# Float32r projections: the two activation parts side by side under one weight load, and three value projections with 512 weight columns

## The chip, the cores and the metric

The kernel runs on one core of a Trainium2 chip. The metric is device time in microseconds (us), the median of several runs. TensorE (PE in the rows) multiplies, VectorE (DVE) and ScalarE (ACT) work on SBUF and PSUM, GpSimd (POOL) takes a few additions, and all large loads are issued from SyncE's queue (SPq).

## The reference, cut to what matters

`x` is [256 tokens, 1024 features], float32. The first block has two layers: layer 0 with a gated convolution beside a retention, layer 1 with a bidirectional state-space scan (S5) followed by a GLU, and each with an MLP of 4096 hidden features. The second block adds three attention-like branches, gates them, and ends in a SwiGLU. What the change touches is this:

```python
# layer 1 of the first block
mix = (z @ w_glu_a) * jax.nn.sigmoid(z @ w_glu_b)            # z = gelu(S5(h)), 1024 -> 1024
x = x + gate_m * mix
h = _rmsnorm(x, norm_g[layer, 1]) * (1.0 + scale_f) + shift_f
x = x + gate_f * (jnp.square(jax.nn.relu(h @ w_fc1[layer])) @ w_fc2[layer])   # 1024 -> 4096 -> 1024
...
# the second block: projections of rmsnorm(x) to gated linear attention (q, k, v, gate),
# to forgetting attention (q, k, v), to memory attention (q), and to 3 x 1024 gates;
# keys and values of a memory of 256 slots; three branch matrices 512 -> 1024, an output
# matrix 1024 -> 1024, and a SwiGLU of 2816 hidden features
```

## The kernel before, in words

Activations lie with a feature to a partition and 256 tokens along the free axis: `[128, 8, 256]` is a whole activation, block `k` of it 128 features. Each float32 matrix product is done with operands of type float32r, in three products. Weights and activations are each split into a high part (ScalarE copies it to float32r, L314) and a low part (VectorE subtracts, L315). `mm3` (L318 to L321) then issues three passes into the same PSUM bank: high weights by high activations, high weights by low activations, low weights by high activations. Each pass streams 256 columns and has its own weight load.

A weight piece is 1 MB, `[128, 8 blocks of 128 inputs, 256 outputs]`. `piece` loads it into one of four buffers (tag `w`) and splits it in four steps, four instructions on ScalarE and four on VectorE, into one of two buffers of high and of low parts (tags `hi`, `lo`). `lin` takes the input blocks `k` in the outer loop and the two output column blocks in the inner one, so a piece is 8 x 2 triples of passes and fills one PSUM bank of 512 columns (two blocks of 256 tokens). Tag `mm` has two such banks, `at` four, `fa` and `fp` one each. `lin_tok` has the roles exchanged: 128 tokens of the activations are the stationary operand and 256 weight columns stream; `tok` (L1154) calls it for value projections, two pieces for 512 columns.

After `lin`, one instruction over both column blocks usually reads the bank: a ReLU (L657) and a square in the MLP, a product with the per-token factor `rb` in the gates (L1290) and in SwiGLU (L1530), `Square` and `Copy` in `heads` (L1172, L1173), a gated product in the branches (L1497), an addition to `x` after `w_out2` (L1505).

The order on each engine is fixed when the program is built: a scheduler simulates the engines and takes what is ready by the order of the source. Some work is traced as fill between the steps of something else: the twelve gate pieces between the steps of the attentions, and the memory's projections (`memory`, L1211) at three places from the GLU on. In GLU the input blocks are taken in the order 0, 2, 4, 6, 1, 3, 5, 7 (`ks`, L1125), since the scan finishes the even ones first. High and low parts of an activation come from a pool `h` of two buffers of 8 KB a partition.

## Time and profile before

| | us |
|---|---|
| median of three runs | 1230.05 (1228.49 to 1230.53) |
| span of the profiled execution | 1227.2 |
| median less span | 2.85 |
| TensorE busy in the span | 1169.7 (95%) |
| VectorE busy | 891.7 (73%) |
| ScalarE busy | 609.7 (50%) |

The busy share of TensorE is the union of its passes with their pipeline time, so a stretch at 100% may still hold more or fewer passes. The span falls into a first half with much loading and scanning (to about 500 us), GLU (500 to 560 us), the second layer's MLP (580 to 770 us), the second block's attentions, branches and output matrix (770 to 1030 us) and SwiGLU (1030 to 1227 us).

### The profile page before, as it was taken

How to read it: one execution, taken by the hardware profiler on the slowest of the kernel's cores; microseconds unless marked ns; L12 is line 12 of the kernel's file. 1: busy time of each engine (PE TensorE's matmuls, PEld its weight loads, DVE VectorE, ACT ScalarE, POOL GpSimd, SP SyncE). 2: the span in 40 equal slices, each digit the busy share in tenths (PEclk: the TensorE clock that was granted, in tenths of full speed). 3: DMA queues.
4: the chain of work that ended last, by engine and by line, in shares of the span. 5: the costliest groups of instructions: out<-in, count | busy, mean ns of one | idle time of the engine just before them, and what ended most of it. 6: DMA issues, size and time to landing. Idle time of an engine off the chain costs nothing. (4 is left out here: it accounts for less than half of the span.)

```text
span 1227.2 us, 25417 instructions
## 1 busy us (share of the span) xinstructions
PE 1169.7 (95%) x10482; PEld 1109.3 (90%) x10482; DVE 891.7 (73%) x1821; ACT 609.7 (50%) x1202; POOL 106.1 (9%) x138
## 2 busy tenths in 40 slices
PE   6899897999999976899999999999999999999998
PEld 4698686999999964899999999999999999999998
DVE  7879888889888859767765656686667686665564
ACT  3577244655555542545544545573465545544441
POOL 0077321000000006200000000000000000000000
PEclk8899997999999977799999999999999999999999
DMA  9888886688888999554466655453443454555541
GB/s 341 340 311 327 297 294 212 238 265 282 297 287 267 300 249 309 216 172 171 169 243 212 233 174 172 164 172 104 151 159 138 172 168 148 194 179 177 194 155 60
DMA packets 69979, 267.29 MB, mean 218 GB/s; under 512 B 7380, under 2 KB 35428, under 8 KB 43240
## 3 DMA queue, kind: packets, MB, share of 16 engines
q1 hardware_dynamic: 69864, 265.68, 63.5%
q8 instruction: 82, 1.34, 0.4%
q14 instruction: 33, 0.27, 0.1%
HBM read 246.85 MB, written 18.81 MB: 216 GB/s over the span
## 5 line engine op out<-in xcount | busy, mean ns | idle before, releaser
L315 DVE TENSOR_TENSOR lo<-w,hi 128x512 fp32r<-128x512 f32 (+1 forms) x640 | 427.6, 712 | 147.7 <-ACT hi L314 147.1
L314 ACT ACTIVATE hi<-w 128x512 fp32r<-128x512 f32 (+1 forms) x640 | 358.4, 625 | 337.0 <-PE mm L320 118.8
L319 PE MATMUL mm<-h,hi 128*128 128x256 f32 x1328 | 379.7, 286 | 0.3 <-ACT h L398 0.3
L320 PE MATMUL mm<-h,hi 128*128 128x256 f32 x1328 | 377.7, 285 | 1.3 <-DVE h L399 1.1
L321 PE MATMUL mm<-h,lo 128*128 128x256 f32 x1328 | 378.6, 285 | 0.0
L319 PEld LDWEIGHTS mm<-h,hi 128*128 128x128 f32 x1328 | 254.7, 192 | 7.2 <-issue 3.4
L320 PEld LDWEIGHTS mm<-h,hi 128*128 128x128 f32 x1328 | 254.6, 192 | 2.8 <-DVE h L399 1.5
L321 PEld LDWEIGHTS mm<-h,lo 128*128 128x128 f32 x1328 | 254.5, 192 | 2.6 <-issue 1.6
L321 PE MATMUL at<-s,lo 128*128 128x256 f32 x720 | 204.4, 284 | 1.7 <-DVE lo L315 1.7
L319 PE MATMUL at<-s,hi 128*128 128x256 f32 x720 | 204.8, 284 | 0.0
L320 PE MATMUL at<-s,hi 128*128 128x256 f32 x720 | 204.1, 284 | 0.0
L321 PEld LDWEIGHTS at<-s,lo 128*128 128x128 f32 x720 | 137.9, 192 | 2.5 <-DVE lo L315 2.1
L319 PEld LDWEIGHTS at<-s,hi 128*128 128x128 f32 x720 | 138.0, 192 | 1.8 <-issue 1.4
L320 PEld LDWEIGHTS at<-s,hi 128*128 128x128 f32 x720 | 138.0, 192 | 0.6 <-issue 0.6
L439 PE MATMUL fa<-wa,crep 128*32 128x256 f32 x704 | 56.4, 428 | 7.0 <-DMA wa<-in_ada_dram 3.8
L537 POOL TENSOR_TENSOR s<-s,cv 128x256 f32<-128x256 f32 x60 | 49.9, 866 | 38.9 <-ACT cv L536 38.7
L439 PEld LDWEIGHTS fa<-wa,crep 128*32 128x32 f32 x704 | 23.0, 120 | 27.0 <-issue 6.4
L319 PE MATMUL fp<-h,hi 128*128 128x256 f32 x144 | 41.9, 291 | 0.7 <-ACT h L314 0.7
L320 PE MATMUL fp<-h,hi 128*128 128x256 f32 x144 | 41.8, 290 | 0.0
L321 PE MATMUL fp<-h,lo 128*128 128x256 f32 x144 | 41.6, 289 | 0.0
L929 ACT COPY Wt<-fp 128x512 f32<-128x512 f32 x32 | 18.6, 581 | 43.3 <-PE fp L928 39.9
L536 ACT ACTIVATE cv<-ap,s 128x256 f32<-128x256 f32 x60 | 29.5, 506 | 17.2 <-POOL s L537 16.4
(438 smaller groups left out, 1829.6 us busy)
## 6 DMA issues: line engine op xcount, KB each, us to landing
w<-in_fc_dram SPq DMA_DIRECT2D x64, 1024.0 KB, 5.1
wa<-in_ada_dram SPq DMA_DIRECT2D x44, 1024.0 KB, 6.5
w<-in_w_in_dram SPq DMA_DIRECT2D x38, 1024.0 KB, 4.9
w<-in_w_gate_dram SPq DMA_DIRECT2D x11, 1024.0 KB, 5.0
w<-in_w_up_dram SPq DMA_DIRECT2D x11, 1024.0 KB, 4.9
Vd<-V SPq DMA_DIRECT2D x16, 512.0 KB, 6.6
w<-in_w_out_dram SPq DMA_DIRECT2D x8, 1024.0 KB, 6.2
Wd<-Wt SPq DMA_DIRECT2D x16, 512.0 KB, 5.2
```

The source lines that it names most:

```text
L314: self.nc.scalar.activation(hi, h, AF.Copy)
L315: self.nc.vector.tensor_tensor(lo, h, hi.bitcast(F32), op=ALU.subtract)
L319: mm(ps, sh, mh, start=start, stop=False, skip_group_check=True)
L320: mm(ps, sh, ml, start=False, stop=False, skip_group_check=True)
L321: mm(ps, sl, mh, start=False, stop=stop, skip_group_check=True)
L439: nc.tensor.matmul(ps[32 * q:32 * q + 32], self.crep[:, 2 * k + k2], w[:, n:n + 256], start=k == 0 and k2 == 0, stop=k == 3 and k2 == 1, t ...
L536: nc.scalar.mul(t, src, w)
L537: nc.gpsimd.tensor_tensor(acc[:, ch], acc[:, ch], t, op=ALU.add)
L929: nc.scalar.copy(W[:, :, k], pt.rearrange("p (e x) -> p e x", e=4))
```

## The change

High and low parts of an activation now lie in one buffer, `[128, 2, 8, 256]`, so that one pass can stream both, 512 columns, under one load of the high weights. The low weights still meet the high part alone, 256 columns, and add to the first half of the bank. A bank then holds one column block in two halves, and their sum is formed on eviction: ScalarE copies the second half to SBUF and VectorE adds it to the first. `lin2` has the column block outside and the input blocks inside. It replaces `lin` in GLU, in the second layer's first MLP matrix, in the memory's keys and in all of the second block and SwiGLU but the last matrix. The first layer, both second MLP matrices, `w_down` and the small projection keep `lin` or `mm3`.

The values of the two attentions and of the memory come from weights laid out with 512 columns (`w_v`, 4 input blocks to a piece): 128 tokens are stationary, 512 weight columns stream, the two token halves in the two `mm` banks at once. In `memory` both value pieces are now one step of the fill. In `ffn` of layer 1 the ReLU is folded into VectorE's square. After `w_out2`, VectorE adds the two halves to `x` one after the other. The pool `h` has one buffer of 16 KB instead of two of 8 KB. Comments and docstrings are gone from the source; the scan's tables share the new `h` buffer.

```diff
+    w2m = np.concatenate([w2[:, :1536], w2[:, 1552:3088], w2[:, 3092:]], 1)
+    d["w_v"] = con(np.concatenate([dense(a, 512) for a in (w2m[:, 512:1024], w2m[:, 2560:3072], f(v["w_mem_kv_2"])[0][:, 512:])]))
...
-        self.vplace = ("h", "w", "hi", "hi", "lo", "h", "lo", "w")
+        self.vplace = ("h2", "w", "hi", "hi", "lo", "h", "lo", "w")
...
+    def lin2(self, W, act, kn=8, cols=(0, 1), tags=("mm", "mm")):
+        for n, c in enumerate(cols):
+            ps = self.pair(tags[n])
+            s = slice(c * 128, c * 128 + 128)
+            for k in range(kn):
+                self.nc.tensor.matmul(ps, W[0][:, k, s], act[2][:, :, k], start=k == 0, stop=False, skip_group_check=True)
+                self.nc.tensor.matmul(ps[:, 0], W[1][:, k, s], act[0][:, k], start=False, stop=k == kn - 1, skip_group_check=True)
+            yield n, ps
+
+    def summed(self, dst, W, act, tags=("mm", "mm")):
+        for c, ps in self.lin2(W, act, tags=tags):
+            self.merge(dst[:, c], ps)
+
+    def merge(self, out, ps):
+        e = self.sb([128, T])
+        self.nc.scalar.copy(e, ps[:, 1])
+        self.nc.vector.tensor_tensor(out, ps[:, 0], e, op=ALU.add)
...
+    def both(self, n=8, tag="h"):
+        a = self.sb([128, 2, n, T], F32R, tag)
+        return a[:, 0], a[:, 1], a
...
     def ffn(self, x, h, l, fill, need, each):
...
-                ps = self.pair()
-                self.lin(ps, self.piece(f"fc1_{l}", 2 * q + j), h, K8)
                 r = self.sb([128, 2, T])
-                nc.scalar.activation(r, ps, AF.Relu)
+                if l:
+                    self.summed(r, self.piece(f"fc1_{l}", 2 * q + j), h)
+                    nc.vector.scalar_tensor_tensor(r, r, 0.0, r, op0=ALU.max, op1=ALU.mult)
...
-        ks = [(k, k) for k in (0, 2, 4, 6, 1, 3, 5, 7)]
...
-            self.lin(pa, Wa, z, ks)
-            self.lin(pb, Wb, z, ks)
-            t = self.sb([128, 2, T])
-            nc.scalar.activation(t, pb, AF.Tanh, scale=0.5)
-            v.scalar_tensor_tensor(t, t, 1.0, pa, op0=ALU.add, op1=ALU.mult)
+            t, a = self.sb([128, 2, T]), self.sb([128, 2, T])
+            self.summed(a, Wa, z)
+            self.summed(t, Wb, z, ("fp", "at"))
+            nc.scalar.activation(t, t, AF.Tanh, scale=0.5)
+            v.scalar_tensor_tensor(t, t, 1.0, a, op0=ALU.add, op1=ALU.mult)
...
-    def tok(self, dst, name, js, h, rc):
-        for n, j in enumerate(js):
-            ps = self.pair()
-            self.lin_tok(ps, self.piece(name, j), h)
-            for b in range(2):
-                self.nc.scalar.activation(dst[:, b, 256 * n:256 * n + 256], ps[:, b], AF.Copy, scale=rc[:, b:b + 1])
+    def tok(self, dst, i, h, rc):
+        ps = [self.ps("mm") for _ in range(2)]
+        for k0 in (0, 4):
+            W = self.piece("w_v", i, k0, 4, 512)
+            for k in range(4):
+                for b in range(2):
+                    s = slice(128 * b, 128 * b + 128)
+                    self.mm3(ps[b], h[0][:, k0 + k, s], h[1][:, k0 + k, s], W[0][:, k], W[1][:, k], k0 + k == 0, k0 + k == 7)
+        for b in range(2):
+            self.nc.scalar.activation(dst[:, b], ps[b], AF.Copy, scale=rc[:, b:b + 1])
...
     def heads(self, dst, name, js, h, g, rc, out=None):
-            ps = self.pair()
-            self.lin(ps, self.piece(name, j), h, [(k, k) for k in range(8)])
+            self.summed(d, self.piece(name, j), h)
             sq = self.sb([128, 2, T], tag="q2")
-            nc.scalar.activation(sq, ps, AF.Square)
-            nc.scalar.activation(d, ps, AF.Copy, scale=g)
+            nc.scalar.activation(sq, d, AF.Square)
+            nc.scalar.activation(d, d, AF.Copy, scale=g)
...
     def memory(self):
-        for n in range(2):
-            self.tok(self.mv[:, :, 256 * n:256 * n + 256], "w_mkv", (2 + n,), (hh, hl), rc)
-            yield
+        self.tok(self.mv, 2, (hh, hl), rc)
+        yield
...
         def gate(i, j):
-            ps = self.pair()
-            self.lin(ps, self.piece("w_in2", 14 + 4 * i + j), h, K8)
             g = gates[i][:, 2 * j:2 * j + 2]
-            tt(g, ps, rb2, op=ALU.mult)
+            self.summed(g, self.piece("w_in2", 14 + 4 * i + j), h)
+            tt(g, g, rb2, op=ALU.mult)
...
                 for c2 in range(2):
-                    ps = self.pair()
-                    self.lin(ps, W, ys[i], [(k, k) for k in range(4)], cols=(2 * c2, 2 * c2 + 1))
+                    z = self.sb([128, 2, T])
+                    for c, ps in self.lin2(W, ys[i], 4, (2 * c2, 2 * c2 + 1)):
+                        self.merge(z[:, c], ps)
-                    v.scalar_tensor_tensor(gates[i][:, s], gates[i][:, s], 1.0, ps, op0=ALU.add, op1=ALU.mult)
+                    v.scalar_tensor_tensor(gates[i][:, s], gates[i][:, s], 1.0, z, op0=ALU.add, op1=ALU.mult)
...
-            self.lin(ps, self.piece("w_out2", j), (mh, ml), K8)
-            v.scalar_tensor_tensor(x[:, 2 * j:2 * j + 2], ps, 0.5, x[:, 2 * j:2 * j + 2], op0=ALU.mult, op1=ALU.add)
+            for c, ps in self.lin2(self.piece("w_out2", j), mx):
+                xc = x[:, 2 * j + c]
+                for a in range(2):
+                    v.scalar_tensor_tensor(xc, ps[:, a], 0.5, xc, op0=ALU.mult, op1=ALU.add)
...
     def swiglu(self, x, h, rb):
-                self.lin(pg, self.piece("w_gate", j0 + j), h, K8)
-                self.lin(pu, self.piece("w_up", j0 + j), h, K8)
+                t, u, w = (self.sb([128, 2, T]) for _ in range(3))
+                self.summed(u, self.piece("w_gate", j0 + j), h)
+                tt(u, u, bc, op=ALU.mult)
                 nc.scalar.activation(t, u, AF.Tanh, scale=0.5)
+                self.summed(w, self.piece("w_up", j0 + j), h, ("fa", "fp"))
                 v.scalar_tensor_tensor(t, t, 1.0, u, op0=ALU.add, op1=ALU.mult)
-                tt(t, t, pu, op=ALU.mult)
+                tt(t, t, w, op=ALU.mult)
...
-            self.pools = {t: pool(t, b) for t, b in (("h", 2), ("s2", self.n2), ("q2", self.nq), ("s1", self.n1), ("s0", 12))}
+            self.pools = {t: pool(t, b) for t, b in (("h", 1), ("s2", self.n2), ("q2", self.nq), ("s1", self.n1), ("s0", 12))}
```

## Rows read from the trace of the kernel before

**Rows 1.** The page: TensorE's granted clock in 40 slices, tenths.

```profile
PEclk8899997999999977799999999999999999999999
```

**Rows 2.** Windows: us, busy us (instructions) of each engine, clock, DMA, GB/s.

```profile
1100.00:1200.00 100.00, 100.00 (x836) 100.00 (x835) 55.64 (x90) 43.75 (x80) 0.00 (x0) 1.00 0.53 178
```

**Rows 3.** Timeline of TensorE in GLU: start us, duration us, instruction; 11 passes apart.

```profile
548.38 0.28 PE L319 MATMUL mm<-h,hi 128*128 128x256 f32 x1
...
549.70 0.28 PE L321 MATMUL mm<-h,lo 128*128 128x256 f32 x1
```

**Rows 4.** Groups by line and shape, TensorE from 500 us on.

```profile
L319 PE MATMUL mm<-h,hi 128*128 128x256 f32 x912 | 259.4, 285 | 0.0
...
L319 PE MATMUL fp<-h,hi 128*128 128x256 f32 x144 | 41.9, 291 | 0.7 <-ACT h L314 0.7
...
L319 PE MATMUL fa<-h,hi 128*128 128x256 f32 x96 | 27.2, 283 | 0.0
L319 PE MATMUL mm<-ys,hi 128*128 128x256 f32 x96 | 27.2, 283 | 0.0
```

**Rows 5.** Timeline of TensorE in cross attention: float32 passes (L1463), then float32r.

```profile
933.57 0.59 PE L1463 MATMUL at<-mk,s 128*128 128x256 f32 x2
934.00 0.38 PE L1438 MATMUL at<-ident,s 128*128 128x128 f32 x2
934.22 0.60 PE L1463 MATMUL at<-mk,s 128*128 128x256 f32 x2
...
934.77 0.28 PE L319 MATMUL mm<-h,hi 128*128 128x256 f32 x1
```

**Rows 6.** Timeline of TensorE in the memory's keys, ten passes apart.

```profile
571.44 0.28 PE L321 MATMUL mm<-hi,mhl 128*128 128x256 f32 x1
...
572.57 0.28 PE L319 MATMUL mm<-hi,mhh 128*128 128x256 f32 x1
```

**Rows 7.** Timeline of TensorE at GLU's start, five passes apart, and the window there.

```profile
505.22 0.41 PE L321 MATMUL fp<-h,lo 128*128 128x256 f32 x1
...
506.29 0.41 PE L320 MATMUL fp<-h,hi 128*128 128x256 f32 x1
...
504.00:509.00 5.00, 5.00 (x25) 5.00 (x24) 3.43 (x13) 2.16 (x5) 0.00 (x0) 0.50 1.01 426
```

**Rows 8.** Groups by line and shape, ScalarE and VectorE from 480 us on.

```profile
L314 ACT ACTIVATE hi<-w 128x512 fp32r<-128x512 f32 x440 | 244.3, 621 | 271.1 <-PE mm L320 101.9 <-issue 84.8 <-PE at L320 57.2
...
L1254 ACT COPY rb<-fp 128x256 f32<-128x256 f32 x1 | 0.4, 372 | 2.3 <-PE fp L369 2.3
...
L315 DVE TENSOR_TENSOR lo<-w,hi 128x512 fp32r<-128x512 f32 x440 | 280.6, 687 | 116.3 <-ACT hi L314 115.9
...
L315 DVE TENSOR_TENSOR lo<-w,hi 128x256 fp32r<-128x256 f32 x4 | 1.4, 418 | 0.0
```

**Rows 9.** Windows: the branches, and the decays with linear attention's projections.

```profile
968.00:1004.40 36.40, 36.40 (x300) 36.22 (x299) 28.56 (x49) 16.17 (x33) 0.00 (x0) 1.00 0.45 153
...
800.00:820.00 20.00, 20.00 (x166) 19.72 (x165) 17.75 (x32) 15.74 (x26) 0.00 (x0) 1.00 0.55 191
```

**Rows 10.** Timeline of VectorE at the end of the scan.

```profile
503.29 1.42 DVE L315 TENSOR_TENSOR h<-s,h 128x256 fp32r<-128x256 f32 x4
...
508.35 1.43 DVE L315 TENSOR_TENSOR h<-s,h 128x256 fp32r<-128x256 f32 x4 [1.57 <-ACT h L314]
```

**Rows 11.** Timeline of VectorE at SwiGLU's start.

```profile
1029.94 2.46 DVE L384 SCALAR_TENSOR_TENSOR h<-x,vec,h 128x256 fp32r<-128x256 f32 x6
1032.31 2.49 DVE L315 TENSOR_TENSOR lo<-w,hi 128x512 fp32r<-128x512 f32 x4
1034.72 0.88 DVE L384 SCALAR_TENSOR_TENSOR h<-x,vec,h 128x256 fp32r<-128x256 f32 x2
```

**Rows 12.** Timeline of ScalarE at the start of block two.

```profile
787.84 0.84 ACT L1161 ACTIVATE s<-mm,rc 128x256 f32<-128x256 f32 x2 [0.61 <-DVE rc L1252]
```

More of the change, by code (lines that the diff above doesn't have):

```diff
@@ L375, in rms @@
         return self.spread(self.rsqrt_eps(ms[:, :, 0]))
+    def both(self, n=8, tag="h"):
+        a = self.sb([128, 2, n, T], F32R, tag)
+        return a[:, 0], a[:, 1], a
     def gained(self, x, g):
-        hh, hl = self.sb([128, 8, T], F32R, "h"), self.sb([128, 8, T], F32R, "h")
+        act = self.both()
+        hh, hl = act[0:2]
         def make(j):
@@ L384, in make @@
                 self.nc.vector.scalar_tensor_tensor(hl[:, c], x[:, c], g[:, c:c + 1], hh[:, c].bitcast(F32), op0=ALU.mult, op1=ALU.subtract)
-        return (hh, hl), make
+        return act, make
     def col(self, name, i=0, n=1):
@@ L393, in normed @@
         nc = self.nc
-        hh, hl = self.sb([128, 8, T], F32R, "h"), self.sb([128, 8, T], F32R, "h")
+        act = self.both()
+        hh, hl = act[0:2]
         for c in range(8):
@@ L1084, in finish @@
             if ih == 0:
-                z.extend(self.sb([128, 8, T], F32R, "h") for _ in range(2))
-            zh, zl = z
+                z.extend(self.both())
+            zh, zl = z[0:2]
             for t2 in range(2):
@@ L1124, in s5 @@
         v.tensor_scalar_mul(hg, self.modv(l, 2), 0.5)
-        ks = [(k, k) for k in (0, 2, 4, 6, 1, 3, 5, 7)]
         for j in range(4):
-            pa, pb = self.pair(), self.pair("fp")
             if j == 0:
@@ L1219, in memory @@
         g = self.col("g_mem", 0, 8)
-        hh, hl = (self.memh.tile([128, 8, T], F32R, name=n) for n in ("mhh", "mhl"))
+        hx = self.memh.tile([128, 2, 8, T], F32R, name="mh")
+        hh, hl = hx[:, 0], hx[:, 1]
         for c in range(8):
@@ L1337, in block2 @@
         gv = self.sb([128, 2, 512])
-        self.tok(gv, "w_in2", (2, 3), h, rc)
+        self.tok(gv, 0, h, rc)
         gs = self.sb([128, 4, T])
         for c in range(2):
-            pg = self.pair()
-            self.lin(pg, self.piece("w_in2", 4 + c), h, K8)
             t, u = self.sb([128, 2, T]), gs[:, 2 * c:2 * c + 2]
-            tt(u, pg, rb2, op=ALU.mult)
+            self.summed(u, self.piece("w_in2", 4 + c), h)
+            tt(u, u, rb2, op=ALU.mult)
             nc.scalar.activation(t, u, AF.Tanh, scale=0.5)
@@ L1347, in block2 @@
         ki, ko = en, eo
-        ps = self.pair()
-        self.lin(ps, self.piece("w_in2", 0), h, K8)
-        v.scalar_tensor_tensor(qi, ps, 0.125, er, op0=ALU.mult, op1=ALU.mult)
-        ps = self.pair()
-        self.lin(ps, self.piece("w_in2", 1), h, K8)
-        tt(ki, ps, en, op=ALU.mult)
-        tt(ko, ps, eo, op=ALU.mult)
+        self.summed(qi, self.piece("w_in2", 0), h)
+        v.scalar_tensor_tensor(qi, qi, 0.125, er, op0=ALU.mult, op1=ALU.mult)
+        kz = self.sb([128, 2, T])
+        self.summed(kz, self.piece("w_in2", 1), h)
+        tt(ki, kz, en, op=ALU.mult)
+        tt(ko, kz, eo, op=ALU.mult)
         P = self.sb([128, 2, 2, 2, 128])
@@ L1386, in block2 @@
         fill.step(self.grate[0])
-        ys = [[self.sb([128, 4, T], F32R, "ys") for _ in range(2)] for _ in range(3)]
+        ys = [self.both(4, "ys") for _ in range(3)]
         for c in range(2):
@@ L1488, in block2 @@
         self.mark("b2.branch")
-        mh, ml = self.sb([128, 8, T], F32R, "h"), self.sb([128, 8, T], F32R, "h")
+        mx = self.both()
+        mh, ml = mx[0:2]
         for n, i in enumerate((0, 1, 2)):
@@ L1668, in build @@
             memh_pool.__exit__(None, None, None)
-            with self.phase(s8=3, s4=self.s4, l2=6, ys=6):
+            with self.phase(s8=3, s4=self.s4, l2=6, ys=3):
                 self.mark("norm2")
```

31 lines of the change are left out of this document (16 added, 15 removed).

## Prediction

> **What bounds the kernel now.** I read the stages before the totals. The page's clock row [rows 1] shows where TensorE ran at half its granted clock: near the start, around 200 us and from about 440 to 520 us, the state-space scan. The change starts after that. From 600 us on TensorE is busy all the time at full clock with 836 passes in 100 us, while VectorE is busy 56 us of it, ScalarE 44, the DMA engines 0.53 [rows 2]. Waits there don't set the end; the number of passes and what each takes do. One pass of 256 columns starts 0.120 us after the one before (11 in 1.32 us [rows 3]); its shown duration of 0.28 us overlaps its neighbours and is no price.
>
> **What is converted.** By the code a piece of 256 output columns is 8 feature blocks by 2 column blocks, 16 triples of three passes. GLU has 8 such pieces, the second layer's fc1 16, the memory's keys 2, the gates 12, linear attention's gate, q and k 4, the heads' projections 6, w_out2 4, gate and up 22; with the 6 branch pieces, also 16 triples each, that is 80 pieces, 1280 triples. The trace's groups agree: 912 + 144 + 96 + 96 and the 32 of the keys [rows 4]. A triple of 256 + 256 + 256 becomes 512 + 256: the same columns, one weight load and one pass fewer.
>
> **Price of a pass of 512.** No row has one of this type. The nearest is the float32 pass of cross attention, which streams for as long at the same clock: two take 0.43 us, and two followed by one float32r pass of 256 take 0.55 [rows 5]. So a long pass is 0.215 with its successor's weight load hidden, the short one 0.12: 0.335 for the pair against 0.360. From below, nothing beats the long row. From above: if a pass is paid by the column at the fastest rate that 256 columns show, 0.113 (ten in 1.13 us [rows 6]), 512 cost 0.226; at the usual rate, 0.240. I take 0.215, because at half clock the period is 0.214 for 256 columns [rows 7], 1.2 columns per ns, exactly the 1.2 GHz level with nothing added, while at 2.4 GHz 256 columns should need half of that, 0.107, and take 0.120. What the extra 0.013 is does not stretch with the array's clock; a weight load that isn't quite hidden behind 256 columns fits, and behind 512 it would be hidden.
>
> The Trainium skill speaks against this: "TensorE: Matmul & The Clock Gate", section "Back-to-back issue gap", gives N / 2.4 + 2.5 ns, so 109 for 256 and 216 for 512 columns; by it a triple falls only from 328 to 325 ns, and 1280 of them give 3 us. The trace agrees for the long pass (0.215) and not for the short (0.120).
>
> **Gains.** 1280 x 0.025 = 32.0 us. The three value projections go from 96 passes of 256 columns (two pieces) to 48 of 512 each: 48 x (0.240 - 0.215) x 3 = 3.6. Together 35.6 us, all in stretches at full clock but for some 5 us of GLU.
>
> **What evictions add.** Each column block now ends in a ScalarE copy out of PSUM (0.37 us) and a VectorE addition (0.42 [rows 8]), where one instruction over two blocks read PSUM before. A block is 8 pairs, 2.68 us. The chain from its last pass is 0.28 + 0.37 + 0.42 and hand-overs, near 1.2 us; its bank is wanted again one block later, 2.68 us on. So 1.5 us remain for what stands ahead in the two queues, mainly pieces of the weight split (0.62 on ScalarE, 0.69 on VectorE, four to a weight piece [rows 8]). That cover is enough where the queues have room; gate/up and GLU alternate over more banks and have more. Seven places have less:
>
> - Branches: 4 feature blocks, so a bank comes back after 1.34 us, close to the 1.2. VectorE is busy 28.6 of 36.4 us there [rows 9]; 24 more additions, 0.40 apart as short ones run in a row [rows 11], make 38, against TensorE's 96 x 0.335 plus some 2 us of attention, 34. I charge 5 us.
> - Decays and linear attention's projections: VectorE 17.75 of 20 us [rows 9]; three to four pieces bring 8 x 0.4 - with 18.6 us to do it in, 2 us over.
> - GLU's start. Before, k runs through the even blocks first, since these come from the scan early; some 24 passes ran on them at half clock [rows 7] while the odd blocks were made (low parts of the two sets from 503.3 and from 508.35 us [rows 10]). lin2 takes k in natural order, so the second pair needs an odd block: TensorE idles to about 508.4 and starts cold (0.214 a pass) what it had begun. 24 warm passes are 2.9 us: 3.
> - SwiGLU's start. lin2 runs all eight k for the first column block at 0.335 each; before, a k lasted 0.72. The normed blocks come at 0.40, the last two at 1034.7 to 1035.6, behind a weight split [rows 11]. 2 us.
> - Value projections hold both "mm" banks from start to end, then both are evicted. The three must wait for the preceding block's additions and, behind them, for a copy of 512 elements (two of 256 take 0.84 [rows 12]): 1 us each, 3.
> - The memory's values are now one step of the fill, so the second piece (its 1 MB load on SP's queue, eight split instructions, its passes) moves from 769 us, where it covered the start of block two, to about 580. There it only shifts work. At 769 TensorE runs into the last normed blocks (0.7 us), and the linear attention's values fill both banks before the per-token factor, that the eviction waits for [rows 12], is ready. 2 us.
> - Elsewhere (heads: square and scale now read the merged tile, one hop later; w_out2: two VectorE reads of each bank): 2 us.
>
> Sum 19 us. The one 16 KB buffer for high and low parts replaces two of 8 KB; both were written and freed together, so I cost it at nothing: the work that hides it is the pass that still reads the old contents, before as after. Loads keep their size; SP's queue issues as many, and 0.53 of the DMA engines leaves room. The ReLU moves from ScalarE to VectorE's squaring (same instruction count there).
>
> 35.6 - 19 = 16.6. The profiled span is 1227.2 us; the median run, 1230.05, lies 2.85 above, which I keep: span 1210.6, time **1213.5 us**.
>
> **Rivals.**
> *All hides*: the scheduler orders the evictions so well that only GLU's start and the branches cost, 8 us: 35.6 - 8 = 27.6, about 1202; with nothing lost, 1194.5. For it: before, TensorE idled for almost nothing [rows 2]. Against: the branches' VectorE sum.
> *Slower passes*: 512 columns at 0.226 to 0.227. A pair costs 0.347, the gain is 1280 x 0.013 + 144 x 0.013 = 18.5, less 19: 1230.5, no change. For it: 0.113 is also a period that rows show [rows 6].
> *Columns are the price* (other side): each column costs 0.120 / 256 whatever the pass; the gain is 0, the list stays: 1249. For it: the rows of this type all have 256 columns, so they can't exclude it. Against: the faster period of the same columns [rows 6]. The page's formula above ends here too: 3 - 19, 1246.
> *Evictions bind* (other side): if the two queues delay a merge by more than the 1.5 us on the 88 blocks outside branches that use only the two "mm" banks, each 0.3 us more is 26 us: 1240. It decides from about 0.2 us a block on. For it: VectorE's extra 0.8 us a piece brings fc1 pieces to some 5 of 5.36 us. Against: fc2 pieces between them have no merges.
>
> **Chances.** Forecast (1205 to 1222) 0.52; all hides 0.14; slower passes 0.12; columns 0.08; evictions 0.14. A measurement of this kernel tells a difference of 0.2% or more, 2.5 us, from none. Faster: 0.52 + 0.14, a third of the slower-pass case and a quarter of the eviction case, 0.74. Same 0.05. Slower 0.21. The range 1198 to 1236 leaves out half of "all hides", the column case and the worse part of the eviction case, 0.2 together. The forecast's own range is 1205 to 1222.
>
> **What would show it.** In fc1 and gate/up stretches, 512-column passes at 0.215 after their start and pairs at 0.335 (0.347 or 0.360 would be the second and third rival). TensorE idle: a gap at 500 to 509 us, one before the first gate piece, waits on VectorE's additions in the branches and next to nothing in fc1. VectorE busy near 85% from 780 us on. If pairs take 0.335 and the time is still over 1225, the list of waits was too short; if fc1's blocks wait for banks, the eviction rival holds.

## The result, and the profile after

The changed kernel takes 1274.45 us (1270.70 to 1279.25), the kernel before on the same chip 1229.27 (1226.64 to 1230.53): ratio 1.0354, 95% interval 1.0328 to 1.0381. It is 45 us slower; the forecast was 1213.5. The profiled span went from 1227.2 to 1268.9.

Four moments divide these 41.7 us: GLU's last addition to `x`, the first and the last gated product of the branches, and the end. Views of the two lines before (L1141, L1497) and after (L1176, L1534); the two times are the first and the last start:

```profile
L1141 DVE SCALAR_TENSOR_TENSOR x<-s,hgate,x x8: 714/726/776, 525.7 to 561.9; 128x256 f32<-128x256 f32 x8
L1497 DVE SCALAR_TENSOR_TENSOR s<-s,mm x12: 679/684/689, 971.6 to 1004.8; 128x512 f32<-128x512 f32 x12
L1176 DVE SCALAR_TENSOR_TENSOR x<-s,hgate,x x8: 734/754/780, 531.4 to 567.7; 128x256 f32<-128x256 f32 x8
L1534 DVE SCALAR_TENSOR_TENSOR s<-s,s x12: 685/691/693, 1001.4 to 1047.1; 128x512 f32<-128x512 f32 x12
```

GLU ends 5.8 us later; from there to the first product it is 24.0 us more; the products take 45.7 us instead of 33.2, 12.5 more; and from the last product to the end it is 0.6 less.

The page of the changed kernel, busy time by engine and the clock row, beside [rows 1]:

```profile
PE 1173.1 (92%) x9058; PEld 1039.3 (82%) x9058; DVE 954.1 (75%) x1997; ACT 657.6 (52%) x1344; POOL 107.5 (8%) x138
...
PEclk9899997999999977997999999999999999999999
```

TensorE is as busy as before with some 1400 passes fewer, and the time is longer, so two things went wrong: the passes are not cheaper as hoped, and TensorE waits. Windows of the changed kernel: GLU's start, the keys, a stretch of fc1, the start of block two, the branches and SwiGLU (columns as in [rows 2]):

```profile
504.00:510.00 6.00, 3.16 (x34) 2.04 (x23) 5.76 (x19) 2.67 (x6) 0.00 (x0) 0.75 0.92 347
570.00:582.00 12.00, 1.43 (x6) 1.05 (x6) 10.44 (x33) 5.24 (x13) 0.00 (x0) 0.58 0.28 104
600.00:700.00 100.00, 99.92 (x672) 91.60 (x672) 68.51 (x131) 49.45 (x97) 0.00 (x0) 1.00 0.58 211
800.00:840.00 40.00, 31.52 (x157) 25.12 (x156) 31.50 (x78) 28.71 (x51) 0.00 (x0) 0.96 0.36 132
1001.40:1047.10 45.70, 38.33 (x192) 30.30 (x191) 35.68 (x67) 22.96 (x51) 0.00 (x0) 0.96 0.34 115
1100.00:1200.00 100.00, 100.00 (x630) 89.87 (x629) 71.17 (x129) 56.56 (x114) 0.00 (x0) 1.00 0.52 186
```

fc1 and SwiGLU have no holes: there the evictions are covered. All the others have: 10.6 of 12 us idle at the keys, 8.5 of 40 at block two's start, 7.4 of 45.7 in the branches, where [rows 9] had none. The branches hold 192 passes as planned.

What TensorE waited for from 500 us on (us in total, times, longest):

```profile
PE mm L341 <- DVE s L353: 10.9, 13, 3.3
PE mm L341 <- DVE mk L353: 6.9, 1, 6.9
PE fp L393 <- DVE rc L1290: 4.3, 1, 4.3
PE at L393 <- DVE s L373: 3.8, 1, 3.8
PE at L1508 <- DVE s L1504: 3.3, 1, 3.3
PE mm L341 <- DVE h L318: 3.0, 2, 1.6
```

L353 is the addition in `merge`, the second half of an eviction; L341 is the 512-column pass. So the largest waits are for a bank whose eviction isn't done. At the keys the rest of the queue shows. Timelines of ScalarE and of VectorE there: both make eight normed blocks first (L429; L428, L430), and only then evict the keys' banks, which TensorE filled long before:

```profile
575.77 3.30 ACT L429 ACTIVATE h<-s,mod 128x256 fp32r<-128x256 f32 x8 [4.45 <-DVE s L428]
578.98 0.75 ACT L352 COPY s<-mm 128x256 f32<-128x256 f32 x2
```

```profile
575.25 3.22 DVE L428 SCALAR_TENSOR_TENSOR s<-x,modg,at 128x256 f32<-128x256 f32 x8 [1.32 <-PE at L393]
578.39 3.25 DVE L430 SCALAR_TENSOR_TENSOR h<-s,mod,h 128x256 fp32r<-128x256 f32 x8
581.56 0.75 DVE L353 TENSOR_TENSOR mk<-mm,s 128x256 f32<-128x256 f32 x2
```

The eviction's own two instructions were priced right (L352 0.363, L353 0.420 us, estimated from [rows 8] as 0.37 and 0.42):

```profile
L352 ACT COPY s<-mm 128x256 f32<-128x256 f32 x134 | 48.5, 363 | 52.5 <-PE mm L342 50.4 <-issue 1.4 <-DVE s L1247 0.5
...
L353 DVE TENSOR_TENSOR s<-mm,s 128x256 f32<-128x256 f32 x128 | 53.6, 420 | 10.5 <-ACT s L352 10.0
```

And the pass. TensorE's timeline in SwiGLU, eleven pairs of 512 and 256 columns apart; it answers [rows 3]:

```profile
1119.68 0.40 PE L341 MATMUL fp<-h,hi 128*128 128x512 f32 x1
1119.92 0.28 PE L342 MATMUL fp<-h,lo 128*128 128x256 f32 x1
...
1123.57 0.40 PE L341 MATMUL mm<-h,hi 128*128 128x512 f32 x1
```

Eleven pairs take 3.89 us, 0.354 each, against 0.360 for three passes before. Over all pairs at full clock the median is 0.350: 0.235 from the long pass's start to the next, 0.117 from the short one's. The forecast had 0.215 and 0.120.

### The profile page after: what moved, and what is told of

Its sections match the earlier page's. It is cut to its first block, busy times and chain, and to the rows that moved or that the text cites. A ratio compares the mean times of both kernels' runs of the same rounds, so it can differ in the third digit from the quotient of the medians.

```text
span 1268.9 us, 22899 instructions
## 1 busy us (share of the span) xinstructions
PE 1173.1 (92%) x9058; PEld 1039.3 (82%) x9058; DVE 954.1 (75%) x1997; ACT 657.6 (52%) x1344; POOL 107.5 (8%) x138
## 4 chain that ended last, share of the span: by engine, by line
PE 77%; DVE 13%; DMA 3%; ACT 3%; POOL 2%; issue 1%; SPq 0%; ACTq 0%; DVEq 0%; POOLq 0%
PE mm L341 18%; PE mm L342 9%; PE at L322 7%; PE at L323 7%; PE at L324 7%; DVE lo L318 5%; PE mm L322 4%; PE mm L323 4%; PE mm L324 4%; PE fp L341 2%; PE fa L470 2%; PE fa L341 2%; DVE fp L564 1%; PE at L170 1%; POOL s L568 1%
## 5 line engine op out<-in xcount | busy, mean ns | idle before, releaser
L318 DVE TENSOR_TENSOR lo<-w,hi 128x512 fp32r<-128x512 f32 (+1 forms) x640 | 436.6, 717 | 173.2 <-ACT hi L317 172.5
L317 ACT ACTIVATE hi<-w 128x512 fp32r<-128x512 f32 (+1 forms) x640 | 363.6, 626 | 272.2 <-PE mm L341 91.8
L341 PE MATMUL mm<-h,hi 128*128 128x512 f32 x912 | 331.4, 405 | 10.3 <-DVE s L353 4.1
L341 PEld LDWEIGHTS mm<-h,hi 128*128 128x128 f32 x912 | 173.1, 190 | 53.6 <-DVE s L353 6.2
L322 PE MATMUL mm<-h,hi 128*128 128x256 f32 x416 | 120.9, 291 | 0.3 <-ACT h L429 0.3
L323 PE MATMUL mm<-h,hi 128*128 128x256 f32 x416 | 119.6, 288 | 1.1 <-DVE h L430 1.1
L322 PEld LDWEIGHTS mm<-h,hi 128*128 128x128 f32 x416 | 80.7, 194 | 6.7 <-issue 3.1
L323 PEld LDWEIGHTS mm<-h,hi 128*128 128x128 f32 x416 | 80.7, 194 | 2.0 <-DVE h L430 1.5
L352 ACT COPY s<-mm 128x256 f32<-128x256 f32 x134 | 48.5, 363 | 52.5 <-PE mm L342 50.4
L353 DVE TENSOR_TENSOR s<-mm,s 128x256 f32<-128x256 f32 x128 | 53.6, 420 | 10.5 <-ACT s L352 10.0
```

What stands on the lines that cost most here:

```text
L317: self.nc.scalar.activation(hi, h, AF.Copy)
L318: self.nc.vector.tensor_tensor(lo, h, hi.bitcast(F32), op=ALU.subtract)
L322: mm(ps, sh, mh, start=start, stop=False, skip_group_check=True)
L323: mm(ps, sh, ml, start=False, stop=False, skip_group_check=True)
L341: self.nc.tensor.matmul(ps, W[0][:, k, s], act[2][:, :, k], start=k == 0, stop=False, skip_group_check=True)
L352: self.nc.scalar.copy(e, ps[:, 1])
```

## Experiments: what a pass costs

**Long passes cut in two.** The changed kernel with each pass of 512 as two of 256 under the same weights; evictions and banks stay.

```diff
-                self.nc.tensor.matmul(ps, W[0][:, k, s], act[2][:, :, k], start=k == 0, ...)
+                for a in range(2):
+                    self.nc.tensor.matmul(ps[:, a], W[0][:, k, s], act[a][:, k], start=k == 0 and a == 0, ...)
```

> The changed kernel with one edit: the pass of 512 columns is issued as two passes of 256 with the same high weights, into the two halves of the bank. Banks, evictions and the order of work are those of the changed kernel. It prices the wide pass alone. Theory P (columns are the price: the changed kernel's pairs take 0.350 us against 0.360 for three narrow passes): at most 1280 x 0.010 = 13 us more, less where TensorE waits anyway, so 1280 to 1288. Rival (the prediction's price, 0.025 a triple, part of it lost in waits): 25 us more or over, 1300 and up.

Measured 1281.98 us, ratio 1.0399 (1.0361 to 1.0437); the span is 11.3 us above the changed kernel's, the ratio 0.0045, 5.5 us. In 100 us of SwiGLU it starts 835 passes, as many as [rows 2]:

```profile
1100.00:1200.00 100.00, 100.00 (x835) 100.00 (x834) 73.44 (x133) 58.00 (x117) 0.00 (x0) 1.00 0.53 182
```

So 1280 long passes are worth some 5 us by the ratios, give or take 6, and 11 by the spans, not 32.

**High weights only.** Left out: the product of low weights and high activations.

```diff
-                self.nc.tensor.matmul(ps[:, 0], W[1][:, k, s], act[0][:, k], start=False, stop=k == kn - 1, ...)
```

> The changed kernel with the passes of low weights left out everywhere but in the value projections, fc2, down and the stages before GLU, so it leaves out the product of low weights and high activations: only the price of a 512-column pass behind another with other weights is read from it, at 2.4 GHz, and its time is that of less work. Columns theory (about 0.115 us per 256 columns whatever stands around them): starts 0.226 to 0.236 apart, median near 0.231. Rival, that a pass of 512 costs 0.215 and the 0.020 more in the changed kernel come from the weight load of the short pass that follows it, or of the long one behind the short: starts 0.213 to 0.219 apart. TensorE then idles between blocks, and VectorE and ScalarE set the pace in the gated stretches: the time should fall less than the 1136 short passes' 133 us, by 70 to 110 us, to 1165 to 1205.

One run, 1171.7 us. Timeline of TensorE, 16 long passes with different weights one behind the other:

```profile
1110.25 3.79 PE L341 MATMUL mm<-h,hi 128*128 128x512 f32 x16
1113.87 0.39 PE L341 MATMUL fa<-h,hi 128*128 128x512 f32 x1
```

3.62 us for 16: 0.226 each; over 1049 such intervals the median is 0.227, the tenth and the ninetieth percentile 0.226 and 0.235. That refutes 0.215. It is twice the 0.113 of [rows 6] (rows of the memory's values, weights streaming past its activations, not of its keys). It can be read in another way: at half clock this run's long passes take 0.427, so 0.213 would be their columns alone at full clock, and 0.013 is over; of the 0.120 for 256 columns the same 0.013 is over beyond 0.107. Whether the extra goes by the column or by the pass, these rows don't tell. The prediction had it gone behind 512 columns, and it is not. Beside a short pass a long one takes a little more, 0.235. The time fell by 103 us, in the range given.

## Experiments: the banks

**Branches and w_out2 alternate over two pairs of banks.**

```diff
-  for c, ps in self.lin2(W, ys[i], 4, (2 * c2, 2 * c2 + 1)):
+  for c, ps in self.lin2(W, ys[i], 4, (2 * c2, 2 * c2 + 1), (("mm", "mm"), ("at", "at"))[c2]):
...
-  for c, ps in self.lin2(self.piece("w_out2", j), mx):
+  for c, ps in self.lin2(self.piece("w_out2", j), mx, tags=(("mm", "mm"), ("at", "at"))[j % 2]):
```

> The changed kernel with one edit: in the branches and the output matrix every second piece half puts its two column blocks into two banks of tag at instead of mm, so four banks take turns. Nothing else is touched. Theory A (a bank now holds one column block, so two banks let TensorE run ahead of the evictions by half as much work as before, and it stops where a weight split stands ahead of a merge): the changed kernel's branches took 45.7 us from the first to the last gated product against 33.2 before; with four banks they should take 35 to 37, and the time fall by 9 to 12 us, to about 1263. Rival B (VectorE and ScalarE simply have too much to do after the added evictions): VectorE is busy as long as before, branches stay above 42 us, time within 4 us of 1274.

1268.23 us, 1.0287 (1.0247 to 1.0328): by the ratios some 8 us less, give or take 6, between the two expectations. The changed kernel's many small waits from 1001 to 1075 us are gone:

```profile
PE mm L341 <- DVE s L353: 7.3, 11, 0.9
```

But a single wait there has grown from 1.3 to 6.0 us. Window of the branches with four banks, and that wait (from 1002 to 1070 us):

```profile
1002.50:1042.00 39.50, 33.47 (x184) 29.10 (x183) 33.82 (x66) 22.04 (x50) 0.00 (x0) 0.93 0.39 135
```

```profile
PE mm L341 <- DVE h L318: 6.0, 1, 6.0
```

VectorE is busy 33.8 of 39.5 us; it ends its work after TensorE has, and w_out2's first operand, the low part made there, comes 6.0 us late. More banks alone don't mend a stage in which VectorE is near its limit.

**Keys into other banks.**

```diff
-  self.heads(self.mk[...], "w_mkv", (n,), (hh, hl, hx), self.col("g_mem_k"), rc)
+  self.heads(self.mk[...], "w_mkv", (n,), (hh, hl, hx), self.col("g_mem_k"), rc, tags=(("at", "at"), ("fa", "fp"))[n])
```

> The changed kernel with one edit: the memory's two key pieces put their column blocks into the banks at, at and fa, fp instead of mm, mm. In the changed kernel TensorE stands idle for 11 us between 570 and 582 us, when both mm banks hold key blocks whose merges are queued behind the norm's chain. Theory A: with banks of their own both key pieces and the values run through this chain; the gap falls under 2 us, the time by 8 to 11 us, to about 1265. Rival C (the gap is due to the values' second piece being moved or to the chain itself being later): the gap stays over 6 us, time over 1270.

1270.91 us, 1.0320 (1.0285 to 1.0356): some 4 us less, which the intervals don't tell from none, where 8 to 11 were expected. The 11 us hole at 570 to 582 is gone, and another stands at 615 us, where the head norm's factors are late (TensorE's waits from 568 to 625 us):

```profile
PE at L393 <- DVE s L1219: 4.3, 1, 4.3
```

**Memory's values last,** where a part of them stood before the change.

```diff
-        self.memat = (1, 3, 0)
+        self.memat = (1, 2, 0)
```

> The changed kernel with the memory's value projection as the last thing before block two instead of in the stretch of the second norm at 570 us. Cover theory (the 4.7 us hole at 806 us, where TensorE waits for both mm banks full of linear attention's values until the per-token factor is ready, is there because nothing is left to cover the second norm's chain): the hole goes or falls under 1 us, the stretch from ffn1's end to the first gate grows by the moved work (about 11 us of passes) less 4, the ffn1 stretch shrinks by about 11; time about 4 us under the changed kernel, 1270.5, with 1268 to 1272.5. Rival, that the factor's chain starts later when the work before it is gone, since VectorE or ScalarE sets it and not TensorE: the hole stays within 1 us and the time within 1.5 us of the changed kernel's.

1276.49 us, 1.0364 (1.0339 to 1.0389): no gain, so the cover theory falls. The wait on the per-token factor `rc` goes as it said, but others of 6.5 and 3.3 us come (its waits, 780 to 840 us). It fits that the second norm's and the decays' chains on VectorE and ScalarE are long by themselves, and that covering their beginning only shows their end; no run tests this alone:

```profile
PE at L1367 <- DVE s L1364: 6.5, 1, 6.5
PE at L1347 <- ACT l L1348: 3.3, 1, 3.3
```

**The value projections alone,** on the kernel before (`tok`, the layout `w_v`, values as one step of the fill).

> The kernel before with one part of the change: the three value projections with 512 weight columns, both token halves in the two mm banks, and the memory's values as one step of the fill. lin stays everywhere else. Theory D (this part costs by itself, since both banks wait for the per-token factor at the start of block two and the cover there was moved): 4 to 8 us slower than before, 1234 to 1238, with a gap near the first eviction of linear attention's values. Rival (it gives its 1 to 4 us of shorter passes): 1226 to 1229.

1236.92 us, 1.0041 (1.0018 to 1.0063), in the range expected, with its longest hole where TensorE waits 4.3 us for `rc`. The values fill both banks before the factor that their eviction needs is ready, as the prediction said of this step, at a higher price: 5.0 us, where its terms (3 and 2, less a gain of 3.6) gave 1.4.

## Experiments: SwiGLU alone loses, and why

**SwiGLU only.** The changed kernel with every other stage's passes, evictions and projections set back.

> The changed kernel with every stage but SwiGLU's gate and up set back to three passes of 256 columns and the old evictions and value projections; the joined buffer for high and low parts stays. Price theory (a triple saves 0.010 us, 352 triples 3.5 us, four banks hide the evictions, and the start loses under 1 us): 1226 to 1230, 2 to 5 us under the kernel before, PE idle in SwiGLU under 2 us. Rival, that the joined 16 KB buffer costs by itself because the next norm's high parts wait for the last pass that reads the old ones: at or over the kernel before, with gaps at the starts of ffn1, block two and SwiGLU. Rival, that the 5.1 us that the SwiGLU stretch was shorter in the changed kernel was a late start cut off elsewhere: within 1 us of the kernel before.

1235.64 us, 1.0028 (1.0015 to 1.0040): slower, where a gain was expected, though SwiGLU itself has no holes once it runs. The rival that the joined buffer costs by itself is the one to follow: two losses stand ahead of it. One is at its start. VectorE and ScalarE, and TensorE's timeline:

```profile
1036.08 1.15 ACT L314 ACTIVATE hi<-w 128x512 fp32r<-128x512 f32 x2 [3.98 <-issue]
1037.14 2.49 ACT L410 ACTIVATE h<-x,vec 128x256 fp32r<-128x256 f32 x6
...
1037.96 2.46 DVE L411 SCALAR_TENSOR_TENSOR h<-x,vec,h 128x256 fp32r<-128x256 f32 x6
...
1038.49 0.50 PE L338 MATMUL mm<-h,hi 128*128 128x512 f32 x1 [1.59 <-DVE h L411]
...
1039.40 0.63 PE L338 MATMUL mm<-h,hi 128*128 128x512 f32 x1
...
1041.32 0.63 PE L338 MATMUL mm<-h,hi 128*128 128x512 f32 x1
```

Two weight splits go ahead of the first normed blocks on ScalarE, and VectorE starts its blocks at 1037.96 behind the same two; in [rows 11] the blocks come first. The hole is small, but behind it three pairs take 1.92 us, 0.64 each, instead of 1.05: TensorE stands at its 1.2 GHz level for 3.4 us. The other loss is 5 us in the scan and at GLU's start, where this kernel's passes are the old ones.

**Joined buffers alone.** The kernel before with one edit: one 16 KB buffer for high and low parts, and for the scan's tables and result with them.

> The kernel before with one edit of the change alone: high and low parts of the activations share one 16 KB buffer (and the scan's tables and z with them); all passes, evictions and projections are the old ones. Buffer theory (z, GELU's result, lies in the joined buffer and waits until the scan's last table in it has been read, where one of two separate buffers came free earlier; GELU of the even blocks then comes some 10 us later and GLU begins on a late operand): scan and GLU end 4 to 6 us later, the rest keeps its length, 1234 to 1238. Rival, as the prediction had it, that the joined buffer costs nothing and the 5 us at GLU of the SwiGLU-only kernel came from elsewhere (order of loads, weight pieces): within 1.5 us of the kernel before.

1238.20 us, 1.0064 (1.0040 to 1.0088). The part that I had put at nothing costs 8 us, with old passes, evictions and projections: 5.9 us to GLU's last addition (567.8 us instead of 561.9), 2.3 at SwiGLU's start. TensorE's waits from 470 to 512 us:

```profile
PE at L1111 <- POOL s L1098: 6.8, 6, 2.0
PE at L1111 <- DMA h<-Vd: 6.6, 4, 4.0
```

**The sixth table elsewhere, GLU even blocks first.** The table goes to the place `hi` in the changed kernel, and GLU takes k in the old order.

```diff
-        self.vplace = ("h2", "w", "hi", "hi", "lo", "h", "lo", "w")
+        self.vplace = ("h2", "w", "hi", "hi", "lo", "hi", "lo", "w")
```

> The changed kernel with the scan's sixth output table moved from the joined buffer to the place of a weight piece's high parts, so that z's buffer is free early, and GLU's passes again even blocks first. Buffer theory: GELU's even blocks come at about 495 us instead of 506, the holes between 500 and 511 us shrink from 6 to under 3 us, GELU ends near 508 and GLU's last addition near 564: 3.5 to 5 us under the changed kernel, 1268 to 1270.5. Rival, that the table's new place is itself late (its slot is held by an earlier table) or that GLU's first weight split waits for it: GELU's end moves by under 1 us and the time by under 1.5 us.

1273.30 us, 1.0351 (1.0326 to 1.0376): nothing. The loads into `h` still hold TensorE up (9.5 us of waits from 470 to 512 us), and that showed the fault: the changed `room` asks whether a place begins with "h", and so does "hi". The third and fourth table, meant for a weight piece's buffer, go to the joined one too, and the edit just tried moved nothing.

**Tables back,** the condition mended, on the joined-buffers-only kernel and on the changed kernel:

```diff
-            if place[0] == "h":
+            if place in ("h", "h2"):
```

> The kernel before with joined buffers as in the joined-buffers-only kernel, and one condition mended: the scan's tables with place hi go to the weight pieces' buffers again. In the change every place that begins with the letter h, hi too, was sent to the joined buffer, so that four of the scan's output tables share one buffer and are loaded one behind the other. Table theory: the waits of TensorE for the loads of these tables (4.0 us at 476, 1.7 at 489 in the joined-buffers-only kernel) go, GELU of the even blocks is back at about 495 us, GLU ends near 563, only the 2.3 us at SwiGLU's start stay: 1232 to 1235. Rival, that z's wait for the whole joined buffer is what costs: GLU still ends 5 us late, 1237 to 1239.

1234.01 us, 1.0006 (0.9992 to 1.0020), against 1.0064 with the old condition. No wait for `h<-Vd` is left, and the additions before GELU begin at 497.92 us for the even and 507.03 for the odd blocks, where the first began at 505.49 with the old condition. GLU's last addition starts at 563.1 instead of 567.8 us. The old condition's row, then the two of this kernel:

```profile
505.49 2.14 DVE L1124 SCALAR_TENSOR_TENSOR s<-s,vec,mm 128x128 f32<-128x128 f32 x8
```

```profile
497.92 2.14 DVE L1124 SCALAR_TENSOR_TENSOR s<-s,vec,mm 128x128 f32<-128x128 f32 x8
507.03 2.14 DVE L1124 SCALAR_TENSOR_TENSOR s<-s,vec,mm 128x128 f32<-128x128 f32 x8
```

> The changed kernel with the same condition mended and nothing else. Table theory: 3 to 6 us below the changed kernel, 1267 to 1271, and now GLU's natural order of k costs what the prediction charged, since the even blocks are early again: a hole of 2 to 3 us at 506 to 509. Rival: within 1.5 us of the changed kernel.

1270.23 us, 1.0303 (1.0277 to 1.0329): by the ratios 6.3 us less than the changed kernel, give or take 4.6. In the profiled executions GLU hardly ends earlier, its last addition starts at 566.9 instead of 567.7 us.

**GLU's even blocks first.** lin2 takes the order of k as an argument; GLU passes (0, 2, 4, 6, 1, 3, 5, 7). On the changed kernel as it is, and with the tables back:

> The changed kernel with GLU's passes taking the even feature blocks first again, as the kernel before did (k order 0, 2, 4, 6, 1, 3, 5, 7). As predicted for this wait: the holes of about 6 us between 500 and 511 us shrink, GLU's first addition to x comes 2 to 4 us earlier, the time falls by about 3 us, to 1270 to 1273. Rival, that the start is set by the scan's last blocks and the first column block needs all eight of them anyway before it can be evicted, so that what the old order gave was that two column blocks of two matrices ran on even blocks at once (four banks): the time falls by under 1.5 us and the rest of the hole stays.

1270.40 us, 1.0327 (1.0296 to 1.0358): less than the interval can tell, and GLU's last addition starts where it did (567.3 us against 567.7). With the even blocks about as late as the odd ones, the order hardly matters.

> The changed kernel with the condition mended and GLU's passes even blocks first. If the prediction's 3 us for GLU's order was right once the even blocks are early: 2 to 4 us below the kernel with the condition mended alone. Rival, that the first column block needs its odd blocks anyway and only two banks are open at a time: 0 to 1.5 us.

1265.58 us, 1.0263 (1.0239 to 1.0286): now it matters, 4.9 us by the ratios, give or take 4.3, and GLU's last addition starts 5.8 us earlier. So neither edit alone moves GLU's end by 1 us, and both together move it by 6.6. GLU's last additions, then the windows at its start, natural order and even first, both with the tables back; the second starts 32 passes in the 6 us, the first 14:

```profile
L1176 DVE SCALAR_TENSOR_TENSOR x<-s,hgate,x x8: 722/754/776, 530.9 to 566.9; 128x256 f32<-128x256 f32 x8
```

```profile
L1177 DVE SCALAR_TENSOR_TENSOR x<-s,hgate,x x8: 733/760/771, 525.4 to 561.1; 128x256 f32<-128x256 f32 x8
```

```profile
504.00:510.00 6.00, 4.48 (x14) 3.11 (x14) 4.68 (x15) 2.48 (x6) 0.00 (x0) 0.50 0.92 377
```

```profile
504.00:510.00 6.00, 6.00 (x32) 5.34 (x31) 4.42 (x15) 2.89 (x7) 0.00 (x0) 0.81 0.99 414
```

## Experiments: which stages may have it

**SwiGLU's first piece old,** sixth table at `hi` (which moved nothing, as shown above).

```diff
+                if j0 + j:
                     self.summed(u, self.piece("w_gate", j0 + j), h)
...
+                    self.lin(ps, self.piece("w_gate", 0), h, K8)
```

> SwiGLU alone on the new passes as in the SwiGLU-only kernel, but its first gate piece in three passes of 256 with k outermost, and the scan's sixth table out of the joined buffer. If the two losses found there (5 us at GLU's start from the joined buffer, 3.6 us at SwiGLU's start from a 1.8 us hole and 3.4 us at half clock behind it) are what ate the gain of some 5 us, both go: 1226 to 1229, 2 to 5 us under the kernel before. Rival, that the start's loss is the order of ScalarE's and VectorE's queues (two weight splits before the first normed block) and not the order of passes: 1230 to 1232, with the hole still there. Rival, that the table's new place costs as much as the old: over 1231.

1235.08 us, 1.0032 (1.0012 to 1.0052): no gain, where 1226 to 1229 was expected. The first loss stays since the table moved nothing. At SwiGLU's start waits of 0.8 and 0.4 us stay with the old passes, as in the joined-buffers-only kernel: so it is the order of splits and norm, the rival, and comes with the joined buffer.

**fc1, gates and SwiGLU,** first pieces of fc1 and SwiGLU old; first with the tables' fault, then with the condition mended.

> As the kernel with SwiGLU's first piece old, and the second layer's fc1 but for its first piece and the twelve gate pieces on the new passes too (240 + 192 triples more); branches, w_out2, keys, heads, linear attention, GLU and the value projections stay as before. If the evictions on two banks are hidden wherever VectorE and ScalarE have room, 432 triples give 0.010 us each, 4.3 us below that kernel: 1222 to 1225. Rival, that fc1's or the gates' blocks wait for their banks (VectorE about 75% busy): no gain or a loss against that kernel, 1226 to 1232, with holes of 0.3 to 1 us ahead of the long passes in 600 to 780 us or among the gates.

1231.34 us, 1.0008 (0.9994 to 1.0022): by the ratios 3.0 us below the kernel with only SwiGLU's first piece old, where 4.3 was expected; the intervals don't quite part the two.

> fc1 (second layer), gates and SwiGLU on the new passes, first pieces of fc1 and SwiGLU old, as in the kernel of that name, with the tables' condition mended instead of the sixth table's place. That kernel was level with the kernel before, 6 us of it lost in scan and GLU. Table theory: these come back, 1224 to 1227, 0.3 to 0.6% under the kernel before. Rival: level again, 1230 to 1233.

1227.07 us, 0.9944 (0.9925 to 0.9964) of the kernel before, 1233.43 on that chip: 6.9 us faster than the kernel before. All its six executions (1223.80 to 1229.13) are shorter than the shortest of 17 of the kernel before there (1230.10). This version beats the kernel before and the changed one. Stretches of 100 us in fc1 and SwiGLU, TensorE without a hole:

```profile
590.00:690.00 100.00, 100.00 (x706) 93.39 (x705) 72.25 (x141) 49.23 (x98) 0.00 (x0) 1.00 0.59 213
1100.00:1200.00 100.00, 100.00 (x680) 92.35 (x679) 65.40 (x116) 52.57 (x103) 0.00 (x0) 1.00 0.52 179
```

48 pieces of 16 pairs at 0.010 us are 7.7 us; less the start's loss of 2.3, 5.4 is what the pass price gives, and the interval (4.4 to 9.2 us) holds it. TensorE has no wait between 507 and 1032 us there, so the gates' evictions are covered too.

**Steps back** from the kernel with tables back and GLU even first: branches and w_out2 old, then keys, heads and the three value projections too.

> The kernel with tables back and GLU even first (1265.6 us), with branches and w_out2 set back to three passes of 256 and one eviction for two column blocks. From the stages: first branch eviction to w_out2's last took 69.3 us there and 57.7 in the kernel before, so 11 to 12 us less, 1253 to 1255.5, with no holes between 1000 and 1050 but those at SwiGLU's start. Rival, that part of these waits is a backlog of VectorE from the gates that the old evictions would meet too: 1257 to 1261.

1252.69 us, 1.0156 (1.0115 to 1.0197): 13.2 us less by the ratios, give or take 6, near the 11 to 12 expected. From 990 to 1054 us TensorE has no hole left:

```profile
990.00:1054.00 64.00, 64.00 (x526) 63.58 (x524) 45.72 (x78) 30.11 (x59) 0.00 (x0) 1.00 0.48 173
```

> The same with the keys, the heads' projections and all three value projections old too; new are GLU, fc1, gates, SwiGLU and linear attention's gate, q and k. If the holes at 570 to 582 (keys, and 13.7 us at half clock behind them), at 801 (values) and at 993 (mq's heads) are these edits alone: 20 to 25 us less than the kernel with the branches old, 1229 to 1234. Rival, that the second norm's chain leaves its holes whatever stands ahead of it, since gates and GLA's projections evict through the same two engines: 1236 to 1242, with holes of over 3 us left at 800 to 840.

1236.37 us, 1.0024 (1.0003 to 1.0044): 16.2 us less, give or take 6, where 20 to 25 were expected. Of the rival's holes small ones stay, 0.9 and 0.6 us at 575 and 581 us, and three of 4.6 us in all from 794 to 808 us, where linear attention's projections meet the second norm's chain.

## Why the prediction was wrong

Two steps failed. The larger is the list of waits, 19 us, with one term in it put at nothing: by the ratios the changed kernel loses 43.5 us, and at the measured prices the passes give back some 14, so the waits and what hangs on them come to some 58 (an estimate from these two). The other is the price of a pass, which was to give 35.6. No rival came near: the highest stood at 1249. By the prediction's own parts:

- **Price of a pass.** The 0.215 of the float32 rows [rows 5] is not the price of a float32r pass of 512: that is 0.226 behind another, 0.235 beside a short one. A pair takes 0.350, so 1280 pairs give 12.8 us, not 32.0. The value projections' long passes, at a median of 0.231 in the changed kernel, give 1.3 and not 3.6. The argument from half clock [rows 7] failed: the extra 0.013 at 2.4 GHz is still there behind 512 columns, so it was no weight load that more columns would hide. The rival "slower passes" had a pair at 0.347; with that rival's price or the measured one, the forecast's own list of 19 us would have led to 1231 to 1236, no gain. The Trainium skill's formula that the prediction weighed ("TensorE: Matmul & The Clock Gate", section "Back-to-back issue gap") came nearer with its estimate of 3 us for the merge; the spacings worked out from it, 109 and 216 ns, are below the 113 and 226 shown here, and the section gives it for isolated passes. That the trace agreed with it on the long pass rested on a float32 row.
- **The joined buffer, at nothing.** By itself it cost 5.9 us by GLU's end, 4.7 of them (567.8 to 563.1) by tables that were sent to it unintended, and 2.3 at SwiGLU's start. I priced the one buffer by the passes that read the activations and did not follow who else takes room under that name.
- **GLU's start, 3.** The mechanism was right, the size 4.9 by the ratios and 5.8 by GLU's end, but it shows only once the tables are back; in the changed kernel as it stands each hides the other.
- **SwiGLU's start, 2.** The size was about right (2.3), by luck, for the reason was wrong: not the order of k, since the old passes lose it too, but two weight splits ahead of the normed blocks.
- **Branches 5, w_out2 in "elsewhere".** 13.2 together. VectorE's sum, 38, was the right bound with four banks (39.5 us from the first to the last product), but two banks add to it: each piece waits some 0.9 and 0.46 us, 45.7 in all. With four the backlog waits at the end.
- **Keys, heads, value projections, 5 with the moved values and some of "elsewhere".** 16.2. The keys were not on the list: their evictions come just when ScalarE and VectorE make the eight normed blocks (the rows above), and TensorE waits 6.9 us with both `mm` banks full. From the keys' test and the values' tests, how much of this is keys, heads or values isn't told apart: the hole moves with each, and on the kernel before the values alone cost 5.0.
- **Evictions in fc1, gates, SwiGLU hidden.** Right: the stretches shown have no holes, which refutes the rival that they bind. VectorE is busy 71% in SwiGLU and 78% in the branches, not the 85% expected.
- **The sum.** Ratios times 1230: the changed kernel 43.5 us over, less 6.3 (tables), 4.9 (GLU's order), 13.2 and 16.2 leaves 3.0 for what remains converted, against -6.9 with GLU, linear attention and the first pieces old too. Each step is uncertain by 4 to 6 us (the intervals' halves taken together); how the 11.2 of the first two divide isn't shown, and in the traces they move GLU's end by 6.6. How the last 10 us divide was not tried; GLU, linear attention's projections and the start of fc1 are in it.

A wait can also cost more than its length, since TensorE stood at half its granted clock in and behind many of them: from 495 us to its last pass 10.7 us before and 34.1 after. But part of that was waiting. It worked 8.9 and 23.0 us of it, so the clock itself costs some 7 of the 41.7 us (an estimate: half the difference, since a pair takes 0.64 us there and 0.35 at full clock). Windows of the changed kernel: the half-clock stretch at the keys, and the sum over all six such stretches:

```profile
571.82:585.47 13.65, 4.57 (x15) 3.83 (x16) 8.93 (x28) 5.28 (x12) 0.00 (x0) 0.50 0.21 77
...
sum 34.12, PE 22.95 PEld 19.38 DVE 22.93 ACT 13.45 POOL 1.17; mean PE 3.83 PEld 3.23 DVE 3.82 ACT 2.24 POOL 0.19
```

The prediction charged this at GLU's start alone.

## What to carry to other kernels

Price a wider pass from passes of the same type, the fastest of them included, and not from another type that streams as long; here merging two of three passes gave back 2.8% of their time. A change that splits one eviction into two pays only where the banks and the slower of the two evicting engines have room, so convert stages one by one and leave the starts and short stages as they are. When two buffers become one, list everything that takes room there by name, tables and scratch too.

## What was not expected of the hardware

A float32r pass of 512 columns takes 0.226 us behind another with other weights, exactly two of the fastest passes of 256 (0.113), and 0.235 when a pass of 256 follows; the float32 rows of [rows 5] run 0.215 at the same clock. In the hole of 11 us at the keys the clock fell to the 1.2 GHz level at 571.8 us, and it rose 3.4 us after TensorE had begun again (582.1 to 585.5).

Small holes were not alike. With SwiGLU alone on the new passes, a hole of 1.6 us, with only eight one-column passes just before it, was followed by 3.4 us at the 1.2 GHz level (0.64 us a pair), from 0.7 us after TensorE had begun again. In the changed kernel a hole of 1.8 us at the same place, behind the same eight passes, was not: from the second on the pairs there take 0.35 us. TensorE's timeline, pairs behind the hole:

```profile
1074.41 0.50 PE L341 MATMUL mm<-h,hi 128*128 128x512 f32 x1 [1.78 <-DVE h L414]
...
1074.86 0.40 PE L341 MATMUL mm<-h,hi 128*128 128x512 f32 x1
...
1075.21 0.40 PE L341 MATMUL mm<-h,hi 128*128 128x512 f32 x1
```
